# Dense expert product of the peer layers: 512 columns of the first tokens fetched, and another order of high parts, low parts and slot sums

## The chip, the cores and the metric

The program runs on one core of one Trainium2 chip. A core has five engines with queues of their own: TensorE (PE; its weight loads are shown as PEld), VectorE (DVE), ScalarE (ACT), GpSimd (POOL) and SyncE (SP), which mostly starts transfers. Sixteen DMA engines move data between the chip's main memory and the core's on-chip memory. The metric is the device time of one execution in microseconds (us); less is better.

## What is computed

The model is a transformer of four blocks on 256 tokens of 1024 numbers: attention with a mixture of experts, a linear recurrence, a first peer layer, a second attention, and a second peer layer. The change is in the peer layers, which run twice. Cut to what matters:

```
def retrieve_chunk(xc):                                   # 128 tokens
    ...                                                   # product keys choose 8 heads x 16 experts of 16384
    expert = e1 * PEER_KEYS + e2
    g = jax.nn.softmax(top_s, axis=-1)
    u = jnp.take(expert_u, expert, axis=0)
    act = jax.nn.gelu(jnp.einsum('thk,td->thk', u, xc))   # a dot product for each chosen expert
    w = (g * act)
    return jnp.einsum('thk,thkd->td', w, jnp.take(expert_v, expert, axis=0))
```

For each token the layer thus adds 128 rows of `expert_v` (16384 rows of 1024 numbers), each with its own weight.

## The kernel before

The function `peer` (L) does one layer. The 256 tokens are two tiles, t = 0 and t = 1, of 128 tokens each (one token on each of 128 partitions). The last stage of the layer is the weighted sum over rows of `expert_v`. It is made in two ways that run side by side.

The dense way: an earlier step (`group`, `build`) has written the weights into `Wt`, for 128 blocks of 128 experts and all 256 tokens, zero where a token did not choose the expert. The loop over the blocks e then multiplies each block's weights with that block's 128 rows of `expert_v` and adds all products up in PSUM, in `dacc`, one for each token tile. So that the product keeps its precision, both factors are split: `K.split` writes a high part on ScalarE (L88) and the rest, the low part, on VectorE (L89), and `dense` (L1942) makes three products, high by high, high weights by low rows, low weights by high rows. `load(e)` starts the transfer of the rows of block e (`vr`, 512 KB, on SP's queue, five blocks ahead); `vparts(e)` makes `vh` and `vl` of them; `wparts(e)` makes `whi` and `wlo` of the weights. `vl` and `vr` share eight buffers of the pool `gp`; `vh`, `whi` and `wlo` have two buffers each in the pool `vp`.

The fetched way: for the first token tile the last DG = 256 of the 1024 columns are left out of the dense product. In their place `slot` fetches, for slot n of 128, the part of the chosen row that belongs to each of the 128 tokens: an indirect transfer `gv`, started by GpSimd (L1693), with the row numbers in `eidh`. `mix` multiplies it by each token's weight and adds it to `gacc`, on VectorE (L1932). So the first token tile has a second matmul of 256 columns beside each of 512.

Each engine runs its instructions in the order in which they are written in the code. A buffer that is used again makes its next writer wait for its last reader. In the loop, the order in the body of block e is: load of e + 5, weights of e + 1, product of e, high and low part of e + 2, one `mix`, and as many `slot` as a count of blocks allows:

```
for e in range(P):
    load(e + AHEAD)
    wparts(e + 1)
    dense(e)
    vparts(e + 2)
    if len(got) > 4 or got and not todo:
        mix()
    while todo and (P - len(todo)) * (P - 12) < (e + 1) * P:
        slot()
```

After the loop the slots that are left are mixed, and `close` multiplies `gacc` and `dacc` by the layer's `gate` (L1947) and adds them to the tokens `x` (L1949).

Of the kernel before, what the change touches and what calls it, by code (L numbers as in the profile page):

```python
# [1378 lines left out]
AHEAD = 5  # L1379
DG = 256  # L1380


def peer(K, L):
    nc, io, sp, tc = K.nc, K.io, K.sp, K.tc
    pre = f"l{L}_peer_"
    with ExitStack() as ctx:
        gp = K.pool(ctx, "gp", 8, side="right")
        fp = K.pool(ctx, "pp")
        px = K.pool(ctx, "px", space=PSUM)
        R = ExitStack()  # L1390
# [151 lines left out]
        ef = rp.tile([P, TK], F32, name="ef")  # L1542
        dots = fp.tile([P, PH, TK], F32, name="dots")
        act = fp.tile([P, 2, PH, TK], F32, name="act")
        ts = fp.tile([P, 2, PH, TK], F32, name="ts")

# [114 lines left out]
        def softmax(t):  # L1661
            d = act[:, t]
            g = ts[:, t]
            nc.vector.tensor_tensor(out=d, in0=g, in1=g[:, :, 0:1].to_broadcast([P, PH, TK]), op=ALU.subtract)
            nc.scalar.activation(g, d, AF.Exp)
            yield
            sm = fp.tile([P, PH], F32, name=f"psm{t}")
            nc.vector.reduce_sum(sm, g, axis=AX.X)
            nc.vector.reciprocal(sm, sm)
            nc.vector.tensor_tensor(out=g, in0=g, in1=sm[:, :, None].to_broadcast([P, PH, TK]), op=ALU.mult)  # L1670
# [3 lines left out]
        def slots(t, w):  # L1674

            e12 = fp.tile([P, 2, P], I32, tag="e12", name="e12")
            f12 = fp.tile([P, 2, PH, TK], F32, tag="f12", name="f12")
            e_ = eid[:, t].rearrange("p a b -> p (a b)")
# [4 lines left out]
            for i, x in enumerate((f12[:, 0], f12[:, 1], w)):  # L1683
                nc.tensor.transpose(ps[:, i, :], x.rearrange("p a b -> p (a b)"), K.ident)
            eT[t] = fp.tile([P, 3, P], F32, name=f"eT{t}")
            nc.scalar.activation(eT[t], ps, AF.Copy)
            e1b[t] = fp.tile([P, P], BF16, name=f"e1b{t}")
            nc.vector.tensor_copy(e1b[t], ps[:, 0])
            ne2[t] = fp.tile([P, P], F32, name=f"ne2{t}")
            nc.vector.tensor_scalar(ne2[t], ps[:, 1], -1.0, None, op0=ALU.mult)  # L1690
# [31 lines left out]

        eidT = fp.tile([P, P], I32, name="eidT")

# [73 lines left out]

        iof = fp.tile([P, P], F32, name="iof")
        nc.gpsimd.iota(iof, pattern=[[1, P]], base=0, channel_multiplier=0, allow_small_or_imprecise_dtypes=True)  # L1800
        io4 = fp.tile([P, P, 4], BF16, name="io4")
        nc.vector.tensor_copy(io4, iof[:, :, None].to_broadcast([P, P, 4]))
# [85 lines left out]
        def vparts(e):  # L1888

            if e < P and e not in his:  # L1890
                his[e] = vp.tile([P, D], F32R, tag="vh", name="vh")
                lo = gp.tile([P, D], F32R, tag="g", name="vl")
                K.split(his[e], lo, rows_[e])
                rows_[e] = lo
# [11 lines left out]
        O.close()  # L1906
        X.close()
        vp = K.pool(ctx, "vp", 2)
        for e in range(2):
            vparts(e)  # L1910


        table = io[pre + "v_2"].rearrange("r (a c) -> (r a) c", c=DG)
        eidh = fp.tile([P, PH, TK], I32, name="eidh")
        nc.vector.tensor_scalar(eidh, eid[:, 0], float(D // DG), float(D // DG - 1), op0=ALU.mult, op1=ALU.add)
        gacc = vp.tile([P, DG], F32, tag="gacc", name="gacc", bufs=1)
# [115 lines left out]
```

## Time and profile before

| | |
|---|---|
| time, median of 3 runs | 2474.07 us (2470.46 to 2477.63) |
| the profiled execution | 2463.86 us, span 2462.1 us |
| busy share of the span | PE 80%, PEld 61%, DVE 71%, ACT 46%, POOL 37% |
| DMA | 673.56 MB, mean 274 GB/s |
| dense stretch, first layer | from 1122.05 us (first matmul of L1942) |
| dense stretch, second layer | to 2448.7 us (start of its last matmul) |

A span is the time from the first to the last instruction of the program. An engine counts as busy while one of its instructions runs; for TensorE instructions overlap, so that its busy share is no measure of how full it is. In rows of the trace "out<-in" names the tile that is written and those that are read, without buffer numbers, "x128" is a count, and what stands behind "<-" at the end of a row is what ended the idle time ahead of it.

### The profile page before, as it was taken

What the parts mean: (1) busy time and instruction counts of PE and PEld (TensorE: products, weight loads), DVE (VectorE), ACT (ScalarE), POOL (GpSimd) and SP (SyncE); (2) the same over time, 40 slices, a digit from 0 to 9 for tenths busy, and PEclk for the clock granted to TensorE, in tenths of its full rate; (3) what the DMA queues carried; (4) which work ended last, traced back from release to release, by engine and by line L of the source; (5) the groups of instructions that cost most, each with busy time, mean ns of one, the idle gap of its engine ahead of it and who ended that gap; (6) DMA issues with size and microseconds to landing.
All of it is one profiled execution on the core that took longest, in us unless ns stands there. A gap on an engine that the chain in (4) does not pass through costs nothing.

```text
span 2462.1 us, 32882 instructions
## 1 busy us (share of the span) xinstructions
PE 1972.2 (80%) x10819; PEld 1499.6 (61%) x10819; DVE 1748.3 (71%) x4122; ACT 1128.2 (46%) x2320; POOL 900.9 (37%) x951
## 2 busy tenths in 40 slices
PE   6997777777884647779999979987555777899997
PEld 3664333356774545557777756866555555677776
DVE  4663121556688979997777775657898999777776
ACT  4451000246412228885555543552222788655553
POOL 2000000100157766763333330005777667333333
PEclk9998888898897779999999989999887989999999
DMA  8649999673678888997888868328888999788885
GB/s 313 215 169 376 419 419 419 197 249 115 190 264 289 304 301 321 347 351 240 255 254 256 256 222 313 134 91 294 278 315 281 337 339 351 255 256 256 256 255 189
DMA packets 203820, 673.56 MB, mean 274 GB/s; under 512 B 23292, under 2 KB 57064, under 8 KB 187258
## 3 DMA queue, kind: packets, MB, share of 16 engines
q1 hardware_dynamic: 112264, 363.92, 42.3%
q0 software_dynamic: 88672, 304.83, 36.1%
q10 hardware_dynamic: 2706, 2.64, 0.3%
q8 instruction: 87, 1.43, 0.2%
q14 instruction: 91, 0.75, 0.1%
HBM read 668.74 MB, written 1.12 MB: 272 GB/s over the span
## 4 chain that ended last, share of the span: by engine, by line
PE 42%; DVE 19%; issue 8%; ACT 6%; DMA 3%; POOL 2%; another core or an unknown queue 1%; ACTq 1%; DVEq 0%; POOLq 0%; SPq 0%
PE dacc L1942 26%; DVE gu L1869 6%; DVE gu L1764 3%; PE gdot L1754 2%; PE pq L1478 2%; POOL gu L1693 2%; DMA gu<-in_l_peer_u_dram,eid 1%; PE wps L1830 1%; DVE o L1815 1%; DMA w<-in_l_ffn_mod_w_dram 1%; PE facc L94 1%; PE facc L96 1%; PE facc L95 1%; PE md L888 1%
## 5 line engine op out<-in xcount | busy, mean ns | idle before, releaser
L89 DVE TENSOR_TENSOR vl<-vr,vh 128x1024 fp32r<-128x1024 f32 x256 | 313.6, 1226 | 170.2 <-ACT vh L88 162.4
L88 ACT ACTIVATE vh<-vr 128x1024 fp32r<-128x1024 f32 x256 | 271.2, 1060 | 308.8 <-PE dacc L1942 307.7
L1693 POOL DMA_INDIRECT gv<-in_l_peer_v_dram,eidh x256 | 245.6, 959 | 446.9 <-DVE gacc L1932 383.0
L1693 POOL DMA_INDIRECT gu<-in_l_peer_u_dram,eidT x256 | 268.1, 1047 | 123.0 <-DVE gu L1869 61.0
L1942 PE MATMUL dacc<-vh,wlo 128*128 128x512 f32 (+1 forms) x1024 | 311.8, 386 | 0.3
L1693 POOL DMA_INDIRECT gu<-in_l_peer_u_dram,eid x256 | 245.4, 958 | 180.9 <-issue 42.2
L1869 DVE SCALAR_TENSOR_TENSOR gu<-gu,xb 128x1024 f32<-128x1024 f32 x256 | 305.7, 1213 | 7.0 <-remote 3.6
L1942 PE MATMUL dacc<-vh,whi 128*128 128x512 f32 (+1 forms) x1024 | 292.1, 366 | 5.8 <-ACT whi L88 5.8
L1942 PE MATMUL dacc<-vl,whi 128*128 128x512 f32 (+1 forms) x1024 | 291.4, 365 | 0.0
L1764 DVE SCALAR_TENSOR_TENSOR gu<-gu,xr 128x1024 f32<-128x1024 f32 x176 | 212.2, 1209 | 19.3 <-DMA gu<-in_l_peer_u_dram,eid 14.8
L1830 PE MATMUL wps<-ow,o 128*128 128x128 f32 x1024 | 158.1, 303 | 74.2 <-ACT o L1826 63.0
L1942 PEld LDWEIGHTS dacc<-vh,wlo 128*128 128x128 f32 x1024 | 172.7, 188 | 71.1 <-DVE wlo L89 37.7
L1830 PEld LDWEIGHTS wps<-ow,o 128*128 128x128 f32 x1024 | 145.7, 211 | 108.8 <-ACT o L1826 85.9
L1754 PE MATMUL gdot<-h,gT 128*128 128x128 f32 x704 | 122.8, 346 | 109.6 <-ACT gT L1749 50.9
L1838 PE MATMUL xb<-x,pair 128*128 128x512 f32 x512 | 181.3, 466 | 22.7 <-DVE gu L1869 13.6
L1942 PEld LDWEIGHTS dacc<-vh,whi 128*128 128x128 f32 x1024 | 175.1, 189 | 39.3 <-ACT whi L88 6.3
L1942 PEld LDWEIGHTS dacc<-vl,whi 128*128 128x128 f32 x1024 | 174.7, 189 | 33.7
L89 DVE TENSOR_TENSOR ws<-w,ws 128x1024 fp32r<-128x1024 f32 (+1 forms) x104 | 120.9, 1176 | 96.1 <-ACT ws L88 96.1
L1754 PEld LDWEIGHTS gdot<-h,gT 128*128 128x128 f32 x704 | 113.5, 253 | 119.3 <-ACT gT L1749 60.0
L764 PE MATMUL gu<-w,XG 128*32 128x256 f32 x1024 | 93.8, 471 | 49.1 <-DMA w<-in_w_up_dram 27.2
L1838 PEld LDWEIGHTS xb<-x,pair 128*128 128x128 f32 x512 | 93.8, 213 | 55.9 <-DVE gu L1869 27.5
L1932 DVE SCALAR_TENSOR_TENSOR gacc<-gv,act,gacc 128x256 f32<-128x256 f32 x254 | 121.5, 479 | 0.9 <-DMA gv<-in_l_peer_v_dram,eidh 0.6
(533 smaller groups left out, 3790.6 us busy)
## 6 DMA issues: line engine op xcount, KB each, us to landing
vr<-in_l_peer_v_dram SPq DMA_DIRECT2D x256, 512.0 KB
w<-in_w_gate_dram SPq DMA_DIRECT2D x32, 1024.0 KB
w<-in_w_up_dram SPq DMA_DIRECT2D x32, 1024.0 KB
w<-in_w_down_dram SPq DMA_DIRECT2D x32, 1024.0 KB
w<-in_l_mix_mod_w_dram SPq DMA_DIRECT2D x24, 1024.0 KB
w<-in_l_ffn_mod_w_dram SPq DMA_DIRECT2D x24, 1024.0 KB
w<-in_l_peer_q_w_dram SPq DMA_DIRECT2D x16, 1024.0 KB
w<-in_l_fox_in_w_dram SPq DMA_DIRECT2D x16, 1024.0 KB
```

Source lines behind the costliest of these rows:

```text
L88: self.nc.scalar.activation(hi, x, AF.Copy)
L89: self.nc.vector.tensor_sub(lo, x, hi.bitcast(F32))
L764: nc.tensor.matmul(gu[s:s + CAP, j * 256:j * 256 + 256], x[:, k, s:s + CAP], W[n, r][:, k, :], start=k == 0, stop=k == 7, tile_position=(0 ...
L1478: nc.tensor.matmul(ps[:, i, c], qw[n][:, k, i * P:i * P + P], h[:, k, c], start=k == 0, stop=k == 7)
L1693: nc.gpsimd.indirect_dma_start(out=dst, out_offset=None, in_=table, in_offset=bass.IndirectOffsetOnAxis(ap=idx, axis=0))
L1754: nc.tensor.matmul(ps, gT[:, k, :], h[:, k, 0:P], start=k == 0, stop=k == 7)
L1764: nc.vector.scalar_tensor_tensor(g_, g_, 1.0, xr[0], op0=ALU.mult, op1=ALU.mult, accum_out=d)
L1830: nc.tensor.matmul(ps[:, q, :], o2[:, q], ow1[:, q], start=True, stop=True)
L1838: nc.tensor.matmul(ps[:, q:q + 512], K.pair[:, j % 64:j % 64 + 1].to_broadcast([P, P]), x1[j // 64][:, q:q + 512], start=True, stop=True)
L1869: nc.vector.scalar_tensor_tensor(g, g, 1.0, xb.pop(0), op0=ALU.mult, op1=ALU.mult, accum_out=dT[:, j:j + 1])
L1932: nc.vector.scalar_tensor_tensor(gacc, g, w, gacc, op0=ALU.mult, op1=ALU.add)
L1942: nc.tensor.matmul(acc[t][:, q, :n], l[:, c], r[:, 512 * q:512 * q + n], start=e == 0 and i == 0, stop=e == P - 1 and i == 2)
```

## The change

DG becomes 512. The first token tile then needs the dense product for its first 512 columns alone, so its second matmul falls away (`if n:`), and each fetched piece, `gv` and `gacc` are twice as wide. `vh` gets three buffers, and the loop makes the parts of block e + 3 in place of e + 2. In the loop `mix` and `slot` stand ahead of `vparts`; a new function `mixed` spreads the 128 mixes over the blocks 2 to 127, so that none is left behind the loop. Five slots are fetched ahead of the loop. To make room, small tiles whose use ends with the build of the weights move from the pool `fp` to a new pool `fq`, which is closed ahead of `vp`; `eidh` is computed earlier, ahead of that build. The gate is fetched at block 122 instead of 119.

```diff
-DG = 256
+DG = 512
@@
-                his[e] = vp.tile([P, D], F32R, tag="vh", name="vh")
+                his[e] = vp.tile([P, D], F32R, tag="vh", name="vh", bufs=3)
@@
         O.close()
         X.close()
+        F.close()
         vp = K.pool(ctx, "vp", 2)
-        for e in range(2):
-            vparts(e)
-
 
         table = io[pre + "v_2"].rearrange("r (a c) -> (r a) c", c=DG)
-        eidh = fp.tile([P, PH, TK], I32, name="eidh")
-        nc.vector.tensor_scalar(eidh, eid[:, 0], float(D // DG), float(D // DG - 1), op0=ALU.mult, op1=ALU.add)
@@
                         n = 512 - (DG if q > t else 0)
-                        nc.tensor.matmul(acc[t][:, q, :n], l[:, c], r[:, 512 * q:512 * q + n], start=e == 0 and i == 0, stop=e == P - 1 and i == 2)
+                        if n:
+                            nc.tensor.matmul(acc[t][:, q, :n], l[:, c], r[:, 512 * q:512 * q + n], start=e == 0 and i == 0, stop=e == P - 1 and i == 2)
@@
+        def mixed(e):
+
+            return max(e - 1, 0) * P // (P - 2)
+
+        for _ in range(5):
+            slot()
+        for e in range(3):
+            vparts(e)
         wparts(0)
         for e in range(P):
             load(e + AHEAD)
             wparts(e + 1)
             dense(e)
-            vparts(e + 2)
-            if len(got) > 4 or got and not todo:
+            for _ in range(mixed(e) - mixed(e - 1)):
                 mix()
-            while todo and (P - len(todo)) * (P - 12) < (e + 1) * P:
-                slot()
-            if e == P - 9:
+                if todo:
+                    slot()
+            vparts(e + 3)
+            if e == P - 6:
                 gate = gate_rows(K, f"l{L}_ffn", gp.tile([P, D], F32, tag="g", name="gate"))
-        while got:
-            mix()
```

How this moves instructions is seen best on VectorE in the steady part of the loop, first layer. Before, with the numbers of the tiles (`vl` is the low part of rows, `wlo` that of weights, `gacc` the slot sum):

```order
L1932 SCALAR_TENSOR_TENSOR gacc_10702<-gv_10757,act_7116,gacc_10702 128x256
L89 TENSOR_TENSOR wlo_10885<-Wt_8737,whi_10884 128x256
L89 TENSOR_TENSOR vl_10901<-vr_10807,vh_10900 128x1024
L1932 SCALAR_TENSOR_TENSOR gacc_10702<-gv_10781,act_7116,gacc_10702 128x256
L89 TENSOR_TENSOR wlo_10910<-Wt_8737,whi_10909 128x256
L89 TENSOR_TENSOR vl_10926<-vr_10832,vh_10925 128x1024
```

The same place of the changed program:

```order
L1932 SCALAR_TENSOR_TENSOR gacc_10698<-gv_10703,act_7119,gacc_10698 128x512
L89 TENSOR_TENSOR vl_10806<-vr_10746,vh_10805 128x1024
L89 TENSOR_TENSOR wlo_10812<-Wt_8740,whi_10811 128x256
L1932 SCALAR_TENSOR_TENSOR gacc_10698<-gv_10705,act_7119,gacc_10698 128x512
L89 TENSOR_TENSOR vl_10828<-vr_10765,vh_10827 128x1024
L89 TENSOR_TENSOR wlo_10834<-Wt_8740,whi_10833 128x256
```

The slot sum has moved from behind `vl` to ahead of it, so that `wlo` follows `vl` at once, and it is twice as wide.

On TensorE, one block of the product before (`dacc_10703` belongs to the first token tile, `dacc_10704` to the second; x2 are two equal rows, for the two halves of the columns):

```order
L1942 MATMUL dacc_10703<-vh_10692,whi_10705 128x512
L1942 MATMUL dacc_10703<-vh_10692,whi_10705 128x256
L1942 MATMUL dacc_10703<-vl_10693,whi_10705 128x512
L1942 MATMUL dacc_10703<-vl_10693,whi_10705 128x256
L1942 MATMUL dacc_10703<-vh_10692,wlo_10706 128x512
L1942 MATMUL dacc_10703<-vh_10692,wlo_10706 128x256
L1942 MATMUL dacc_10704<-vh_10692,whi_10705 128x512 x2
L1942 MATMUL dacc_10704<-vl_10693,whi_10705 128x512 x2
L1942 MATMUL dacc_10704<-vh_10692,wlo_10706 128x512 x2
```

One block of the changed program:

```order
L1943 MATMUL dacc_10699<-vh_10711,whi_10723 128x512
L1943 MATMUL dacc_10699<-vl_10712,whi_10723 128x512
L1943 MATMUL dacc_10699<-vh_10711,wlo_10724 128x512
L1943 MATMUL dacc_10700<-vh_10711,whi_10723 128x512 x2
L1943 MATMUL dacc_10700<-vl_10712,whi_10723 128x512 x2
L1943 MATMUL dacc_10700<-vh_10711,wlo_10724 128x512 x2
```

The three matmuls of 256 columns are gone, and nine of 512 are left.

At the head of the stage, VectorE before had two low parts and the index product ahead of the first `wlo`:

```order
L89 TENSOR_TENSOR vl_10693<-vr_10659,vh_10692 128x1024
L89 TENSOR_TENSOR vl_10697<-vr_10661,vh_10696 128x1024
L1915 TENSOR_SCALAR eidh_10700<-eid_7113 128x128
L89 TENSOR_TENSOR wlo_10706<-Wt_8737,whi_10705 128x256
L89 TENSOR_TENSOR wlo_10712<-Wt_8737,whi_10711 128x256
```

The changed program has three low parts there:

```order
L89 TENSOR_TENSOR vl_10712<-vr_10664,vh_10711 128x1024
L89 TENSOR_TENSOR vl_10716<-vr_10666,vh_10715 128x1024
L89 TENSOR_TENSOR vl_10720<-vr_10668,vh_10719 128x1024
L89 TENSOR_TENSOR wlo_10724<-Wt_8740,whi_10723 128x256
L89 TENSOR_TENSOR wlo_10730<-Wt_8740,whi_10729 128x256
```

The first `wlo` now stands behind one more low part, and the index product has moved to an earlier stage.

## Rows read from the trace of the kernel before

**Rows 1.** The page, part 4: the chain that ended last, by line.
```profile
PE dacc L1942 26%; DVE gu L1869 6%; DVE gu L1764 3%; PE gdot L1754 2%; PE pq L1478 2%; POOL gu L1693 2%; DMA gu<-in_l_peer_u_dram,eid 1%; PE wps L1830 1%; DVE o L1815 1%; DMA w<-in_l_ffn_mod_w_dram 1%; PE facc L94 1%; PE facc L96 1%; PE facc L95 1%; PE md L888 1%
```

**Rows 2.** Windows: length, busy of PE, PEld, DVE, ACT, POOL, clock, DMA share, GB/s.
```profile
1300.00:1400.00 100.00, 100.00 (x468) 78.94 (x467) 75.96 (x118) 53.28 (x78) 36.85 (x39) 1.00 0.84 256
```

**Rows 3.** Groups from 1150 to 1430 us: count, busy us, mean ns, idle before.
```profile
L89 DVE TENSOR_TENSOR vl<-vr,vh 128x1024 fp32r<-128x1024 f32 x109 | 133.6, 1225 | 67.3 <-ACT vh L88 65.4 <-issue 2.0
...
L88 ACT ACTIVATE vh<-vr 128x1024 fp32r<-128x1024 f32 x110 | 116.6, 1060 | 132.9 <-PE dacc L1942 132.9
...
L1693 POOL DMA_INDIRECT gv<-in_l_peer_v_dram,eidh x110 | 104.4, 949 | 178.7 <-DVE gacc L1932 175.4 <-issue 3.3
...
L1932 DVE SCALAR_TENSOR_TENSOR gacc<-gv,act,gacc 128x256 f32<-128x256 f32 x109 | 52.1, 478 | 0.0
```

**Rows 4.** Timeline around 1300 us: start, duration, engine, line, idle before.
```profile
1300.79 1.06 ACT L88 ACTIVATE vh<-vr 128x1024 fp32r<-128x1024 f32 x1 [1.18 <-PE dacc L1942]
...
1301.89 1.22 DVE L89 TENSOR_TENSOR vl<-vr,vh 128x1024 fp32r<-128x1024 f32 x1 [0.59 <-ACT vh L88]
...
1303.03 0.48 DVE L1932 SCALAR_TENSOR_TENSOR gacc<-gv,act,gacc 128x256 f32<-128x256 f32 x1
1303.19 0.51 PE L1942 MATMUL dacc<-vh,whi 128*128 128x512 f32 x2
...
1303.43 0.42 DVE L89 TENSOR_TENSOR wlo<-Wt,whi 128x256 fp32r<-128x256 f32 x1
1303.53 0.51 PE L1942 MATMUL dacc<-vl,whi 128*128 128x512 f32 x2
...
1303.90 0.62 PE L1942 MATMUL dacc<-vh,wlo 128*128 128x512 f32 x2
...
1304.36 0.64 PE L1942 MATMUL dacc<-vh,whi 128*128 128x512 f32 x2
...
1305.30 0.63 PE L1942 MATMUL dacc<-vh,wlo 128*128 128x512 f32 x2
...
1305.97 1.06 ACT L88 ACTIVATE vh<-vr 128x1024 fp32r<-128x1024 f32 x1 [1.22 <-PE dacc L1942]
```

**Rows 5.** The page, part 5: two wider forms, from the stage before.
```profile
L1693 POOL DMA_INDIRECT gu<-in_l_peer_u_dram,eidT x256 | 268.1, 1047 | 123.0 <-DVE gu L1869 61.0
...
L1869 DVE SCALAR_TENSOR_TENSOR gu<-gu,xb 128x1024 f32<-128x1024 f32 x256 | 305.7, 1213 | 7.0 <-remote 3.6
```

**Rows 6.** Windows of full transfers: first row loads, gathered 4 KB rows, weight loads.
```profile
1112.00:1116.00 4.00, 3.36 (x23) 2.65 (x21) 3.93 (x8) 3.27 (x11) 0.00 (x0) 1.00 0.97 387
1000.00:1050.00 50.00, 37.84 (x204) 29.50 (x205) 49.73 (x100) 44.13 (x134) 35.73 (x34) 0.93 0.97 350
246.00:308.00 62.00, 45.63 (x366) 21.32 (x366) 10.35 (x20) 4.29 (x10) 0.00 (x0) 0.82 1.01 419
```

**Rows 7.** Timeline at the head of the first layer's dense stage.
```profile
1119.70 1.99 ACT L88 ACTIVATE vh<-vr 128x1024 fp32r<-128x1024 f32 x2
1120.78 2.36 DVE L89 TENSOR_TENSOR vl<-vr,vh 128x1024 fp32r<-128x1024 f32 x2 [3.48 <-ACT vh L88]
...
1123.67 1.01 PE L1942 MATMUL dacc<-vh,wlo 128*128 128x512 f32 x2
```

**Rows 8.** Timeline at the end of the second layer's dense stage.
```profile
2448.42 0.62 PE L1942 MATMUL dacc<-vh,wlo 128*128 128x512 f32 x2
2449.82 0.48 DVE L1932 SCALAR_TENSOR_TENSOR gacc<-gv,act,gacc 128x256 f32<-128x256 f32 x1 [0.35 <-DMA gv<-in_l_peer_v_dram,eidh]
2450.34 0.42 DVE L1947 TENSOR_TENSOR gacc<-gacc,gate 128x256 f32<-128x256 f32 x1
2450.68 2.21 DVE L1947 TENSOR_TENSOR gtmp<-dacc,gate 128x512 f32<-128x512 f32 x4
...
2452.81 0.87 DVE L1949 TENSOR_TENSOR x<-gacc,x 128x256 f32<-128x256 f32 x1
2453.60 1.28 DVE L1949 TENSOR_TENSOR x<-gtmp,x 128x512 f32<-128x512 f32 x2
```

More of the change, by code (lines that the diff above doesn't have):

```diff
@@ L1388, in peer @@
         fp = K.pool(ctx, "pp")
+        F = ExitStack()
+        fq = K.pool(F, "fq", side="right")
         px = K.pool(ctx, "px", space=PSUM)
@@ L1542, in peer @@
         ef = rp.tile([P, TK], F32, name="ef")
-        dots = fp.tile([P, PH, TK], F32, name="dots")
+        dots = fq.tile([P, PH, TK], F32, name="dots")
         act = fp.tile([P, 2, PH, TK], F32, name="act")
-        ts = fp.tile([P, 2, PH, TK], F32, name="ts")
+        ts = fq.tile([P, 2, PH, TK], F32, name="ts")
         def top16(jobs):
@@ L1666, in softmax @@
             yield
-            sm = fp.tile([P, PH], F32, name=f"psm{t}")
+            sm = fq.tile([P, PH], F32, name=f"psm{t}")
             nc.vector.reduce_sum(sm, g, axis=AX.X)
@@ L1674, in slots @@
         def slots(t, w):
-            e12 = fp.tile([P, 2, P], I32, tag="e12", name="e12")
-            f12 = fp.tile([P, 2, PH, TK], F32, tag="f12", name="f12")
+            e12 = fq.tile([P, 2, P], I32, tag="e12", name="e12")
+            f12 = fq.tile([P, 2, PH, TK], F32, tag="f12", name="f12")
             e_ = eid[:, t].rearrange("p a b -> p (a b)")
@@ L1684, in slots @@
                 nc.tensor.transpose(ps[:, i, :], x.rearrange("p a b -> p (a b)"), K.ident)
-            eT[t] = fp.tile([P, 3, P], F32, name=f"eT{t}")
+            eT[t] = fq.tile([P, 3, P], F32, name=f"eT{t}")
             nc.scalar.activation(eT[t], ps, AF.Copy)
-            e1b[t] = fp.tile([P, P], BF16, name=f"e1b{t}")
+            e1b[t] = fq.tile([P, P], BF16, name=f"e1b{t}")
             nc.vector.tensor_copy(e1b[t], ps[:, 0])
-            ne2[t] = fp.tile([P, P], F32, name=f"ne2{t}")
+            ne2[t] = fq.tile([P, P], F32, name=f"ne2{t}")
             nc.vector.tensor_scalar(ne2[t], ps[:, 1], -1.0, None, op0=ALU.mult)
@@ L1721, in rows @@
                 yield
-        eidT = fp.tile([P, P], I32, name="eidT")
+        eidT = fq.tile([P, P], I32, name="eidT")
         def second():
@@ L1796, in peer @@
         R.close()
-        iof = fp.tile([P, P], F32, name="iof")
+        iof = fq.tile([P, P], F32, name="iof")
         nc.gpsimd.iota(iof, pattern=[[1, P]], base=0, channel_multiplier=0, allow_small_or_imprecise_dtypes=True)
-        io4 = fp.tile([P, P, 4], BF16, name="io4")
+        io4 = fq.tile([P, P, 4], BF16, name="io4")
         nc.vector.tensor_copy(io4, iof[:, :, None].to_broadcast([P, P, 4]))
@@ L1808, in peer @@
         slots(0, act[:, 0])
-        wT[0], wT[1] = eT[0][:, 2], fp.tile([P, P], F32, name="wT1")
-        dT = fp.tile([P, P], F32, name="dT")
+        wT[0], wT[1] = eT[0][:, 2], fq.tile([P, P], F32, name="wT1")
+        dT = fq.tile([P, P], F32, name="dT")
+        eidh = fp.tile([P, PH, TK], I32, name="eidh")
+        nc.vector.tensor_scalar(eidh, eid[:, 0], float(D // DG), float(D // DG - 1), op0=ALU.mult, op1=ALU.add)
         def group(t, j, dve):
@@ L1955, in peer @@
             dense(e)
-            vparts(e + 2)
-            if len(got) > 4 or got and not todo:
+            for _ in range(mixed(e) - mixed(e - 1)):
                 mix()
-            while todo and (P - len(todo)) * (P - 12) < (e + 1) * P:
-                slot()
-            if e == P - 9:
+                if todo:
+                    slot()
+            vparts(e + 3)
+            if e == P - 6:
                 gate = gate_rows(K, f"l{L}_ffn", gp.tile([P, D], F32, tag="g", name="gate"))
-        while got:
-            mix()
         close((0, slice(D - DG, D), gacc, gacc, nc.vector),
               *((t, slice(512 * q, 512 * q + 512 - (DG if q > t else 0)), acc[t][:, q, :512 - (DG if q > t else 0)], gp.tile([P, D], F32, tag="g", name="gtmp")[:, :512 - (DG if q > t else 0)], (nc.gpsimd, nc.vector)[t])
-                for t in range(2) for q in range(2)))
+                for t in range(2) for q in range(2) if DG < 512 or q <= t))
 RATE = 160
```

## The prediction

> **What bounds the kernel now.** I read the page's chain first. The matmuls that sum the dense expert product (L1942) are the largest piece of what ended last [rows 1], and they run in two stretches, one in each peer layer. The windows come next: in a stretch away from both ends TensorE is busy without a gap at full clock (1.00, the 2.4 GHz level), VectorE is busy three quarters of the time, and the DMA engines show a share of 0.84 at 256 GB/s [rows 2]. That looks like a TensorE bound. It isn't one: matmuls overlap, so a busy PE hides waits of the order of a tenth of a microsecond.
>
> The groups of the stretch say more. 109 low parts in 280 us make 280/109 = 2.57 us for a block of 128 experts. ScalarE is idle 133 us of the 280, and all of that ends with a matmul of L1942; VectorE is idle 67 us, nearly all ended by ScalarE's `vh`; GpSimd waits for the slot sums [rows 3]. ScalarE waits for TensorE, VectorE for ScalarE, so the question is whether TensorE waits for VectorE, which would close a ring. The timeline shows it does [rows 4]. One turn, from `vh` of one block to `vh` two blocks on (there are two buffers of `vh`, so the ring carries every other block):
> - `vh` 1300.79 to `vl` 1301.89: 1.10
> - `vl` to the slot sum `gacc` at 1303.03: 1.14
> - `gacc` to `wlo` at 1303.43: 0.40
> - `wlo` (0.42 long) to the first matmul with `wlo` at 1303.90: 0.47
> - from there to the second tile's matmuls at 1304.36: 0.46 (one of 512 columns that had stood waiting, one of 256)
> - 1304.36 to the last pair's start at 1305.30: 0.94 (two pairs of 512)
> - last pair to the next `vh` at 1305.97: 0.67
>
> The sum is 5.18 us for two blocks, 2.59 a block, which is the measured period within 0.02. So the ring sets the pace: end of the product, high part, low part, slot sum, low part of the weights, end of the product two blocks on.
>
> **The steady block after the change.** Three edits touch this ring.
> - *The slot sum moves ahead of the low part.* VectorE now runs `wlo`, `gacc`, `vl`, so between `vl` and the next `wlo` nothing stands: minus 0.40. The sum falls into the time in which VectorE waits for `vh`. It is twice as wide; the same operation took 478 ns on 256 columns [rows 3] and 1213 ns on 1024 [rows 5], 0.957 ns a column, so 512 take 478 + 245 = 723 ns and hold VectorE 0.40 + 0.245 = 0.645. VectorE then needs 1.14 + 0.645 and 0.34 to 0.42 for `wlo` (with or without the 0.08 by which `gacc`'s 0.48 overlapped its successor), 2.13 to 2.21 a block. If that cover were gone (a block under 2.2) it would itself be the bound.
> - *512 columns are fetched.* The 256-column matmuls of the first token tile go, three a block. Without a stall a pair of 512 + 256 takes 1303.53 - 1303.19 = 0.34 and a pair of 512 takes 0.94/2 = 0.47 or, before a break, 0.46, so a 256 costs 0.34 - 0.23 = 0.11. Only the one behind `wlo` lies in the ring: 0.46 becomes 0.35 (from below 0.23, if the waiting matmul loses its start-up; from above 0.46). Minus 0.11.
> - *Three buffers of `vh`, made three blocks ahead.* I cost this at nothing in the ring. The high part of block e+3 still waits for the product of block e, and `wlo` of block e+2 stands behind the low part of block e+3 on VectorE, so the same two-block ring passes through other names. Before, block e+2's own high part was in it; now the part is made a block earlier than needed, but the queue keeps it in.
>
> The new turn: 1.10 + 1.14 + 0.47 + 0.35 + 0.94 + 0.67 = 4.67 us, 2.335 a block, 0.255 less than by the same rows before. Taken from 2.57 it gives 2.31. TensorE alone needs nine matmuls at 0.23 and the start-up, 2.07 + 0.11 = 2.18, so it still waits about 0.13. GpSimd's issue took 949 ns [rows 3] and stays below half the block; I take it unchanged for rows twice as long, because the same instruction for rows of 1024 columns took 1047 ns [rows 5]; it would need 2.31 us to count.
>
> The ring holds some 125 of the 128 blocks, and the first three or four blocks before had no slot sum in it yet, so the gain is 125 x 0.255 - 0.5 = 31.4 us a layer.
>
> **The transfers.** A block brings 512 KB of rows and, now, 128 x 2 KB instead of 128 x 1 KB of gathered rows: 786 KB instead of 655 KB, which in 2.31 us is 340 GB/s. The trace of before has no such mixture at that rate. Nearest rows: 387 GB/s where the first row loads of this very stretch queue up behind gathers, 350 GB/s where gathers of 4 KB rows run alone, 419 for weight loads [rows 6]. I take the first for the row loads and the second for the gathered rows: 524/387 + 262/350 = 1.35 + 0.75 = 2.10 us, under 2.31 by a tenth, hidden. The bounds are 786/419 = 1.88 and, from the share, the second rival. The Trainium skill, "DMA: Bandwidth & Descriptors", section Specifications, speaks against the change here: it gives a core about 358 GB/s from HBM, by which I estimate 2.20 us a block and the same sum with half the margin; the trace's 387 and 419 already lie above that figure.
>
> **Head and tail of each layer.** Three high and low parts now stand ahead of the first weights instead of two. ScalarE's two took 1.99, VectorE's two 2.36, the second of them 1.14 [rows 7]; a third `vl` puts the first `wlo` 1.14 later, and the small index product (0.13 of VectorE's queue there) has moved to the stage before, where it costs about as much as it saves. The first matmul with `wlo` stood at 1123.67; it comes 1.0 later. Bounds: 0.93 (a third high part, 1.99 - 1.06, if ScalarE's work were what counts) and 1.14. The five gathers issued first find GpSimd idle.
>
> At the end, before, the last product pair ended at 2448.42 + 0.62 = 2449.04, but the last slot sum waited for its gather until 2449.82, and the gated sum came at 2450.34; the last add ended at 2454.88, 5.84 behind the product [rows 8]. Now the slot sums end inside the loop and their gating ahead of the product's end; three products of 512 follow (2.21 less the 256 one, about 1.88), the add of the 512 columns (0.87 for 256, plus 0.245), and 1.28 for two adds, with 0.2 of overlap: 4.1. Minus 1.7 a layer; bounds 0.8 (only the wait goes) and 2.5. The gate's load is issued three blocks nearer the end, still some 14 us ahead of its use.
>
> **Sum.** 2 x (31.4 - 1.0 + 1.7) = 64.2 us. The profiled execution took 2463.86 us (its span is 2462.1), so 2399.7. The median of the three runs shown is 2474.07, 10.2 above that execution; the same difference from it gives 2410 us, 2.6% less. About 0.3% (7.4 us) is what a measurement of this kernel tells from no change.
>
> **The rivals.**
> - *The ring opens, and VectorE sets the pace.* If the stall's start-up goes with the stall (0.23 in place of 0.35) and the two interleaved rings fall in step, the block comes down to VectorE's 2.13 to 2.21. At 2.17 it saves 0.40 x 251 + 1.4 = 102 us: 2372. For it: the turn is only 0.15 above that floor. Against: nothing in the order takes `vl` out from ahead of `wlo`.
> - *The transfers set the pace, and it ends slower.* The place is the wait of `vh` for its rows. If the share of 0.84 at 256 GB/s [rows 2] were work that doesn't overlap, the engines would give 256/0.84 = 305 GB/s and a block need 786/305 = 2.58 us, about level with before. A little less, 300 GB/s, makes 2.62: 0.05 x 252 + 2 for the heads = 15 us more, with nothing left of the tail's gain because the last gathers come late: 2489. It decides from where the mixture gets less than 786/2.57 = 306 GB/s. For it: the share is high while nobody waits for a transfer. Against: 387 GB/s at a share of 0.97 [rows 6], so a share overstates what a transfer needs.
> - *Between the two:* the mixture gets 306 to 340 GB/s, most of the gain is lost. At 320, 2.46 a block, it saves 0.11 x 251 + 1 = 29: 2445.
> - *No change:* the ring is longer by another wait that the rows don't show (the `gacc` of 512 holding VectorE so long that `vl` comes late, 1.0 instead of 0.645): 2.52 and more, some 2460 to 2480.
>
> **How the numbers follow.** The forecast has 0.62, with a block of 2.25 to 2.38 and its own range 2392 to 2426. The opened ring 0.11, transfers in between 0.13, slower by transfers 0.09, no change 0.05. The range leaves out the slower end and the deepest part of the first rival: 2375 to 2452. Faster by over 0.3%: 0.62 + 0.11 + 0.13 + 0.01 of the last = 0.87; within 0.3%: 0.04; slower 0.09.
>
> **What would show it.** In the windows of the dense stretch 43 low parts in 100 us instead of 39, the clock still at 1.00, DMA at about 340 GB/s. In the timeline `wlo` directly behind `vl`, `gacc` behind `wlo`, ended before the next `vh` is. ScalarE's `vh` should still be released by a matmul: that is the ring. If `vh` is released by the transfer of its rows, or `gacc` by its gather, the second or third rival has come. If VectorE has no idle time ahead of `vl`, the first has. At the end, the gated sum should stand ahead of the last matmul. The prediction is wrong above all if the mixture of row loads and gathers doesn't reach 340 GB/s.

## The result and the profile after

The changed kernel takes 2404.84 us (median of 4 runs, 2401.21 to 2416.12); the kernel before, run on the same chip, 2472.27. The ratio is 0.9733, with a 95% interval of 0.9696 to 0.977: 2.7% faster, where 2.6% was forecast. Its profiled execution took 2404.95 us with a span of 2403.2, so the profiled spans differ by 58.9 us.

The windows of the changed kernel: length, busy time of PE, PEld, DVE, ACT, POOL, granted clock, DMA share, GB/s. The first two lie at the head of the first layer's dense stage, the third well inside it; 2230 to 2330 us in the second layer shows the same (VectorE 94%, 341 GB/s).

```profile
1120.00:1125.00 5.00, 1.17 (x3) 0.50 (x2) 3.33 (x3) 4.04 (x6) 3.91 (x3) 0.50 0.48 139
1125.00:1130.00 5.00, 4.55 (x12) 3.52 (x12) 0.83 (x3) 1.05 (x2) 3.06 (x3) 0.50 0.97 340
1300.00:1390.00 90.00, 86.31 (x349) 62.29 (x349) 84.69 (x117) 52.90 (x78) 50.47 (x39) 1.00 0.97 340
```

Beside [rows 2], VectorE went from 76% busy to 94%, the transfers from 256 to 340 GB/s, and PE from 100% to 96%: with less work to cover it, the wait for the low part of the weights is now seen as idle time of the multiplying engine. The page says so too. This is its chain by line; in [rows 1] the product had 26% of it.

```profile
PE dacc L1943 10%; DVE gu L1873 7%; ACT vh L88 5%; DVE gu L1766 4%; DVE wlo L89 2%; PE gdot L1756 2%; PE pq L1480 2%; DVE o L1819 1%; DMA w<-in_l_ffn_mod_w_dram 1%; PE facc L94 1%; ACT ow L1828 1%; DMA gu<-in_l_peer_u_dram,eid 1%; POOL gu L1695 1%; PE facc L96 1%
```

The groups of the changed kernel from 1150 to 1390 us, which answer to [rows 3]: 104 low parts in 240 us are 2.31 us a block (one part more or less at an edge is 0.02). ScalarE still waits for the product alone and the weight load for `wlo`: the ring is still there. VectorE's idle time ahead of `vl` fell from 67 us in 280 to 14 in 240.

```profile
L1695 POOL DMA_INDIRECT gv<-in_l_peer_v_dram,eidh x105 | 138.2, 1316 | 105.5 <-DVE gacc L1932 101.6 <-DVE wlo L89 3.1 <-issue 0.6
L89 DVE TENSOR_TENSOR vl<-vr,vh 128x1024 fp32r<-128x1024 f32 x104 | 127.8, 1229 | 14.3 <-ACT vh L88 14.3
...
L88 ACT ACTIVATE vh<-vr 128x1024 fp32r<-128x1024 f32 x103 | 109.3, 1061 | 99.8 <-PE dacc L1943 99.8
...
L1943 PEld LDWEIGHTS dacc<-vh,wlo 128*128 128x128 f32 x309 | 57.8, 187 | 52.1 <-DVE wlo L89 43.0
```

One turn of that ring, from the timeline of the changed kernel (start, duration, engine, idle time before it), as in [rows 4]:

```profile
1300.76 1.21 DVE L89 TENSOR_TENSOR vl<-vr,vh 128x1024 fp32r<-128x1024 f32 x1
...
1301.10 1.69 POOL L1695 DMA_INDIRECT gv<-in_l_peer_v_dram,eidh  x1 [1.58 <-DVE gacc L1932]
...
1302.14 1.06 ACT L88 ACTIVATE vh<-vr 128x1024 fp32r<-128x1024 f32 x1 [1.16 <-PE dacc L1943]
...
1303.23 1.26 DVE L89 TENSOR_TENSOR vl<-vr,vh 128x1024 fp32r<-128x1024 f32 x1 [0.27 <-ACT vh L88]
1303.24 0.95 POOL L1695 DMA_INDIRECT gv<-in_l_peer_v_dram,eidh  x1 [0.45 <-DVE gacc L1932]
...
1304.42 0.41 DVE L89 TENSOR_TENSOR wlo<-Wt,whi 128x256 fp32r<-128x256 f32 x1
1304.75 0.74 DVE L1932 SCALAR_TENSOR_TENSOR gacc<-gv,act,gacc 128x512 f32<-128x512 f32 x1
1304.88 0.50 PE L1943 MATMUL dacc<-vh,wlo 128*128 128x512 f32 x1 [0.19 <-DVE wlo L89]
1305.22 0.62 PE L1943 MATMUL dacc<-vh,whi 128*128 128x512 f32 x2
...
1306.15 0.62 PE L1943 MATMUL dacc<-vh,wlo 128*128 128x512 f32 x2
...
1306.80 1.06 ACT L88 ACTIVATE vh<-vr 128x1024 fp32r<-128x1024 f32 x1 [1.16 <-PE dacc L1943]
```

`vh` to `vl` 1.09, `vl` to `wlo` 1.19, `wlo` to the first matmul with it 0.46, to the second tile's matmuls 0.34, to the last pair 0.93, to the next `vh` 0.65: 4.66 us for two blocks. The forecast had 1.10, 1.14, 0.47, 0.35, 0.94 and 0.67, 4.67. `gacc` stands directly behind `wlo`, and in one block of two `vl` still waits (0.27) for its high part, in the other (1300.76, 1305.42) it follows `gacc` at once. So VectorE is idle for only 0.27 of the 4.66: its own limit lies just below the ring.

The head of the first layer's dense stage, timeline of the changed kernel:

```profile
1120.59 2.94 ACT L88 ACTIVATE vh<-vr 128x1024 fp32r<-128x1024 f32 x3
...
1123.88 0.80 PE L1943 MATMUL dacc<-vh,whi 128*128 128x512 f32 x1 [3.83 <-ACT whi L88]
...
1125.55 0.80 PE L1943 MATMUL dacc<-vh,wlo 128*128 128x512 f32 x1 [0.45 <-DVE wlo L89]
1126.14 1.06 PE L1943 MATMUL dacc<-vh,whi 128*128 128x512 f32 x2
...
1127.00 1.06 PE L1943 MATMUL dacc<-vl,whi 128*128 128x512 f32 x2
...
1128.95 1.06 ACT L88 ACTIVATE vh<-vr 128x1024 fp32r<-128x1024 f32 x1 [4.81 <-PE dacc L1943]
```

And the first high part that a product released in the kernel before, from its timeline at the same place, with one of its windows there (columns as above):

```profile
1126.41 1.06 ACT L88 ACTIVATE vh<-vr 128x1024 fp32r<-128x1024 f32 x1 [4.11 <-PE dacc L1942]
...
1125.00:1130.00 5.00, 5.00 (x26) 4.19 (x25) 1.62 (x3) 2.52 (x4) 4.01 (x4) 0.98 0.55 176
```

From the first `vh` to the first matmul with `wlo` is now 4.96 us; in [rows 7] it was 3.97. To the end of the first product it is 8.36, where it was 1126.41 - 1119.70 = 6.71.

The end of the second layer's dense stage in the changed kernel, which answers to [rows 8]:

```profile
2389.49 2.32 DVE L1932 SCALAR_TENSOR_TENSOR gacc<-gv,act,gacc 128x512 f32<-128x512 f32 x3
...
2391.84 0.69 DVE L1948 TENSOR_TENSOR gacc<-gacc,gate 128x512 f32<-128x512 f32 x1
2391.94 0.61 PE L1943 MATMUL dacc<-vh,wlo 128*128 128x512 f32 x2
2392.45 1.88 DVE L1948 TENSOR_TENSOR gtmp<-dacc,gate 128x512 f32<-128x512 f32 x3
...
2394.25 0.79 DVE L1950 TENSOR_TENSOR x<-gacc,x 128x512 f32<-128x512 f32 x1
2394.96 1.28 DVE L1950 TENSOR_TENSOR x<-gtmp,x 128x512 f32<-128x512 f32 x2
```

The slot sums and their gating are done before the product ends at 2392.55; the last add ends 3.69 us later, where it was 5.84.

By stages, from the starts and ends in the two timelines (dense: first `vh` to the end of the last matmul; tail: from there to the last add):

| us | before | after | difference |
|---|---|---|---|
| dense, first layer | 332.97 | 304.62 | -28.4 |
| dense, second layer | 332.79 | 303.63 | -29.2 |
| two tails | 11.61 | 7.38 | -4.2 |
| all the rest | | | +2.8 |
| span | 2462.1 | 2403.2 | -58.9 |

The rest lies outside the dense stages and tails, where the change moves little but the index product; whether these 2.8 us are its doing or the spread between two executions, no run shows.

### The profile page after: what moved, and what is told of

The parts are those of the page before. It is cut to its first block, busy times and chain, and to the rows that moved or that the text cites. A ratio compares the mean times of both kernels' runs of the same rounds, so it can differ in the third digit from the quotient of the medians.

```text
span 2403.2 us, 31336 instructions
## 1 busy us (share of the span) xinstructions
PE 1893.5 (79%) x10051; PEld 1396.2 (58%) x10051; DVE 1809.0 (75%) x4120; ACT 1129.1 (47%) x2320; POOL 990.2 (41%) x949
## 4 chain that ended last, share of the span: by engine, by line
PE 25%; DVE 23%; issue 14%; ACT 12%; DMA 3%; POOL 2%; another core or an unknown queue 2%; ACTq 1%; DVEq 0%; SPq 0%; POOLq 0%
PE dacc L1943 10%; DVE gu L1873 7%; ACT vh L88 5%; DVE gu L1766 4%; DVE wlo L89 2%; PE gdot L1756 2%; PE pq L1480 2%; DVE o L1819 1%; DMA w<-in_l_ffn_mod_w_dram 1%; PE facc L94 1%; ACT ow L1828 1%; DMA gu<-in_l_peer_u_dram,eid 1%; POOL gu L1695 1%; PE facc L96 1%
## 5 line engine op out<-in xcount | busy, mean ns | idle before, releaser
L1695 POOL DMA_INDIRECT gv<-in_l_peer_v_dram,eidh x256 | 334.1, 1305 | 284.5 <-DVE gacc L1932 231.9
L1943 PE MATMUL dacc<-vh,wlo 128*128 128x512 f32 x768 | 281.3, 420 | 25.3 <-DVE wlo L89 25.3
L1943 PE MATMUL dacc<-vh,whi 128*128 128x512 f32 x768 | 262.1, 395 | 7.7 <-ACT whi L88 7.7
L1943 PE MATMUL dacc<-vl,whi 128*128 128x512 f32 x768 | 261.3, 394 | 0.0
L1943 PEld LDWEIGHTS dacc<-vh,wlo 128*128 128x128 f32 x768 | 144.5, 188 | 129.3 <-DVE wlo L89 106.2
L1932 DVE SCALAR_TENSOR_TENSOR gacc<-gv,act,gacc 128x512 f32<-128x512 f32 x254 | 188.1, 740 | 0.2
L1943 PEld LDWEIGHTS dacc<-vl,whi 128*128 128x128 f32 x768 | 145.2, 189 | 33.6
L1943 PEld LDWEIGHTS dacc<-vh,whi 128*128 128x128 f32 x768 | 145.7, 190 | 30.5 <-ACT whi L88 8.1
```

The source lines that it names most:

```text
L1695: nc.gpsimd.indirect_dma_start(out=dst, out_offset=None, in_=table, in_offset=bass.IndirectOffsetOnAxis(ap=idx, axis=0))
L1932: nc.vector.scalar_tensor_tensor(gacc, g, w, gacc, op0=ALU.mult, op1=ALU.add)
```

## The experiments

My theory is that the pace is the two-block ring: product, high part, low part, low part of the weights, product. The rivals are a plain saving of matmul work (three narrow matmuls less a block), a third buffer that does the work, and transfers that limit the changed kernel. The first four runs were made on one chip, where the kernel before took 2427.75 us (10 runs, 2419.45 to 2433.6), the last four on another, where it took 2426.96 (7 runs, 2420.53 to 2432.34). Ratios are to the kernel before on the same chip, and what a ratio is in microseconds is against its time there. The changed kernel itself was not run on these chips; it enters by its ratio above, 0.9733, whose interval is 0.0037 to either side, so where a difference is small I go by the length of the dense stages and tails in the traces. The first four edits are against the changed kernel.

**The order alone.** 256 columns fetched and two buffers, as before, with the slot sum ahead of the low part. What else the change moves stays as in the changed kernel: the slot sums spread over the blocks, five gathers ahead of the loop, the index product.

```diff
-DG = 512
+DG = 256
-                his[e] = vp.tile([P, D], F32R, tag="vh", name="vh", bufs=3)
+                his[e] = vp.tile([P, D], F32R, tag="vh", name="vh", bufs=2)
-        for e in range(3):
+        for e in range(2):
-            vparts(e + 3)
+            vparts(e + 2)
```

> The slot sum ahead of the low part, but 256 columns fetched and two buffers of the high part, made two blocks ahead. Theory (a ring of two blocks through high part, low part, low part of the weights and product): the turn loses the 0.40 us of the slot sum, 5.18 - 0.40 = 4.78, 2.39 a block; but with twelve matmuls TensorE needs 9 x 0.23 + 3 x 0.11 = 2.40 without a stall and 2.51 with one in every block, so the block comes down from 2.57 to 2.40 to 2.50 only: 20 to 45 us faster than before, 2427 to 2452. Rival (the order makes the whole gain): 2.31 a block, about 2405. Rival (fewer matmuls make it, the order nothing): 2.57, about 2470.

Measured: 2381.99 us, ratio 0.9821 (0.9787 to 0.9855), 45.8 us less, at the upper end of the 20 to 45 expected. Its two tails are 3.87 us each, so some 4 of the 45.8 come from the spread of the slot sums and not from the order. Its window (columns as above):

```profile
1250.00:1350.00 100.00, 100.00 (x497) 84.53 (x496) 81.16 (x125) 56.69 (x84) 41.48 (x43) 1.00 0.87 272
```

and two of its groups from 1150 to 1350 us:

```profile
L89 DVE TENSOR_TENSOR vl<-vr,vh 128x1024 fp32r<-128x1024 f32 x83 | 101.8, 1227 | 37.8 <-ACT vh L88 37.8
...
L1943 PE MATMUL dacc<-vh,wlo 128*128 128x512 f32 x248 | 84.3, 394 | 0.0
```

A block takes 200/83 = 2.41 us, and no matmul with `wlo` waits: the ring would now allow (5.18 - 0.40)/2 = 2.39, and twelve matmuls, nine of them 0.23 and three 0.11, need 2.40. The order brings the ring down to what TensorE has to do, where it ends.

**Everything but the order.** 512 columns and three buffers, with the low part ahead of the slot sum again.

```diff
+            vparts(e + 3)
             for _ in range(mixed(e + 1) - mixed(e)):
                 ...
-            vparts(e + 3)
```

> The changed kernel with the slot sum put back behind the low part of the rows; 512 columns and three buffers stay. Theory: the sum of 512 holds VectorE 0.67 us between the low part of the rows and that of the weights, so the two-block turn grows from 4.66 to 5.33, 2.66 a block: 0.35 x 250 = 87 us slower than the changed kernel, about 2490, slower than before by some 20. Rival (three buffers have opened the ring, so the place of the sum counts for nothing): 2.31 a block, about 2405. Rival (nine matmuls in place of twelve are what pays): at most 2.4 a block, about 2430.

Measured: 2440.29 us, ratio 1.0056 (1.0038 to 1.0075): slower than before, by 12.5 us where some 20 were expected. Its window:

```profile
1250.00:1350.00 100.00, 85.85 (x339) 60.38 (x337) 83.97 (x115) 51.41 (x75) 36.42 (x38) 1.00 0.90 300
```

and its groups from 1150 to 1350 us:

```profile
L89 DVE TENSOR_TENSOR vl<-vr,vh 128x1024 fp32r<-128x1024 f32 x76 | 93.2, 1226 | 32.4 <-ACT vh L88 32.4
L1943 PE MATMUL dacc<-vh,wlo 128*128 128x512 f32 x227 | 84.5, 426 | 25.3 <-DVE wlo L89 25.3
```

200/76 = 2.63 us a block. TensorE has three matmuls fewer than in the kernel before and is slower: the longer sum (0.66 from its start to that of `wlo`, instead of 0.40) stands between `vl` and `wlo`, and the ring waits for it. A plain saving of matmul work, as the whole of the gain, falls with this run. PE now shows 14% of idle time where the kernel before, with nearly the same pace, showed none.

**Two buffers.** The changed kernel with the high parts made two blocks ahead.

```diff
-                his[e] = vp.tile([P, D], F32R, tag="vh", name="vh", bufs=3)
+                his[e] = vp.tile([P, D], F32R, tag="vh", name="vh", bufs=2)
-        for e in range(3):
+        for e in range(2):
-            vparts(e + 3)
+            vparts(e + 2)
```

> The changed kernel with two buffers of the high part, made two blocks ahead; order and 512 columns stay. Theory: the two-block turn has the same parts, high part, low part, low part of the weights, product, so 2.31 a block as in the changed kernel; the head of each layer is shorter by one low part, 1.0 us and up to 1.6 with the clock's later rise: 2 to 3 us faster, 2402 and within 0.3% of it. Rival (the third buffer pays): the block goes back by a good part of the 0.26 gained, 2.45 and more, 2440 and above.

Measured: 2358.55 us, ratio 0.9726 (0.9693 to 0.9759), as the changed kernel's 0.9733. A dense stage and its tail together take 307.8 us in the first layer and 307.4 in the second, 308.3 and 307.3 in the changed kernel: the shorter head that was expected is there, but the tail is 1.0 longer. Groups from 1150 to 1350 us:

```profile
L89 DVE TENSOR_TENSOR vl<-vr,vh 128x1024 fp32r<-128x1024 f32 x86 | 106.1, 1234 | 11.3 <-ACT vh L88 11.3
...
L1943 PEld LDWEIGHTS dacc<-vl,whi 128*128 128x128 f32 x257 | 48.1, 187 | 34.7 <-DVE vl L89 22.2
```

2.32 us a block. The weight load now waits mostly for `vl` instead of `wlo`, but the turn is as long. The third buffer brings nothing in this change.

**The weights' parts two blocks ahead.** If `wlo` behind the low part is what holds the ring closed, it opens when each `wlo` is made a block earlier.

```diff
-                ws[e] = [vp.tile([P, T], F32R, tag=n, name=n) for n in ("whi", "wlo")]
+                ws[e] = [vp.tile([P, T], F32R, tag=n, name=n, bufs=3) for n in ("whi", "wlo")]
         wparts(0)
+        wparts(1)
-            wparts(e + 1)
+            wparts(e + 2)
```

> The changed kernel with the parts of the weights made two blocks ahead (three buffers of each), so that the low part of the weights of block e+3 and not e+2 stands behind the low part of the rows of block e+3. Theory: the ring now spans three blocks and its turn of about 4.7 us makes 1.6 a block, so it no longer counts; VectorE sets the pace with 1.14 + 0.33 + 0.67 = 2.14 us a block, TensorE needs 2.07: 2.15 to 2.2 a block, 28 to 40 us faster than the changed kernel, 2365 to 2377. Rival (the transfers are the limit already, the DMA share in the changed kernel is 0.96 to 0.97 at 338 GB/s): 2.31 a block stays, about 2405.

Measured: 2315.94 us, ratio 0.954 (0.9508 to 0.9572). That is 0.0193 x 2427 = 47 us below the changed kernel, more than the 28 to 40 expected. Its window:

```profile
1250.00:1350.00 100.00, 100.00 (x424) 75.46 (x423) 100.00 (x141) 63.99 (x95) 85.66 (x48) 1.00 0.99 368
```

its groups from 1150 to 1350 us:

```profile
L1695 POOL DMA_INDIRECT gv<-in_l_peer_v_dram,eidh x95 | 172.4, 1814 | 29.0 <-issue 28.4 <-DMA gv<-in_l_peer_v_dram,eidh 0.6
L89 DVE TENSOR_TENSOR vl<-vr,vh 128x1024 fp32r<-128x1024 f32 x94 | 115.4, 1227 | 0.0
L1943 PE MATMUL dacc<-vh,wlo 128*128 128x512 f32 x282 | 100.3, 410 | 0.0
```

and its timeline on VectorE:

```profile
1251.05 0.42 DVE L89 TENSOR_TENSOR wlo<-Wt,whi 128x256 fp32r<-128x256 f32 x1
...
1251.38 0.75 DVE L1932 SCALAR_TENSOR_TENSOR gacc<-gv,act,gacc 128x512 f32<-128x512 f32 x1
...
1252.04 1.22 DVE L89 TENSOR_TENSOR vl<-vr,vh 128x1024 fp32r<-128x1024 f32 x1
...
1253.18 0.42 DVE L89 TENSOR_TENSOR wlo<-Wt,whi 128x256 fp32r<-128x256 f32 x1
```

VectorE runs without a gap: 0.33 + 0.66 + 1.14 = 2.13 us a block, and no matmul or weight load waits for `wlo`. The ring is open and VectorE sets the pace, at the lower end of the 2.13 to 2.21 that the first rival had. It costs something at the end: VectorE is late there, and the tail is 5.5 us instead of 3.7.

**VectorE or the transfers.** The version with the weights two blocks ahead, with the slot sum over 64 of the 512 fetched columns; everything is still fetched.

```diff
+        nc.vector.memset(gacc, 0.0)
-                nc.vector.tensor_scalar(gacc, g, w, None, op0=ALU.mult)
+                nc.vector.tensor_scalar(gacc[:, :64], g[:, :64], w, None, op0=ALU.mult)
-                nc.vector.scalar_tensor_tensor(gacc, g, w, gacc, op0=ALU.mult, op1=ALU.add)
+                nc.vector.scalar_tensor_tensor(gacc[:, :64], g[:, :64], w, gacc[:, :64], op0=ALU.mult, op1=ALU.add)
```

> The kernel with the weights two blocks ahead, and the slot sum over 64 of its 512 columns (the other 448 columns of the first tokens' fetched part are left out of the result; all rows are still fetched). VectorE then needs about 1.14 + 0.33 + 0.25 = 1.7 us a block. Theory (in that kernel VectorE is the limit, and the transfers at 370 GB/s are not): TensorE takes over with nine matmuls at 0.23, 2.07 to 2.1 a block in place of 2.13, and the transfers reach 375 to 380 GB/s: 8 to 15 us faster, ratio to the kernel before 0.948 to 0.951. Rival (the transfers are the limit, their share is 0.99 to 1.00): the block stays at 2.13 and the ratio at 0.954.

Measured: 2291.38 us, ratio 0.9454 (0.9426 to 0.9482), below what was expected. Its window:

```profile
1250.00:1350.00 100.00, 100.00 (x443) 82.81 (x442) 85.94 (x148) 66.96 (x98) 80.60 (x51) 1.00 1.01 389
```

and its groups from 1150 to 1350 us (the product is L1944 here):

```profile
L88 ACT ACTIVATE vh<-vr 128x1024 fp32r<-128x1024 f32 x98 | 104.0, 1062 | 66.0 <-PE dacc L1944 50.3 <-DMA vr<-in_l_peer_v_dram 13.1 <-DVE gacc L1933 1.5
...
L1944 PE MATMUL dacc<-vh,wlo 128*128 128x512 f32 x295 | 98.8, 389 | 0.0
```

200/98.5 = 2.03 us a block, with no wait on TensorE: nine matmuls at 0.226, its own floor. The same row loads and gathers come at 389 GB/s, so in the version before it VectorE was the limit and the transfers were not. The waits of `vh` for its rows grow here to 13 of its 66 us, from 4 of 73.

**A slower gather issue: the slot sum in PSUM.** GpSimd's issue grew from 949 ns [rows 3] to 1316 in the changed kernel and 1814 with the weights ahead. I suspected the slot sum, whose operands both lie in SBUF, the core's on-chip memory; this run puts `gacc` into PSUM, in the version with the weights two blocks ahead.

```diff
-        gacc = vp.tile([P, DG], F32, tag="gacc", name="gacc", bufs=1)
+        gacc = K.pool(ctx, "pg", space=PSUM).tile([P, DG], F32, name="gacc")
```

> The kernel with the weights two blocks ahead, and the slot sum kept in PSUM, so that its instruction reads one operand and not both from SBUF. GpSimd's issue of a gather took 949 ns before the change, 1305 after it and 1814 with the weights two ahead, while VectorE's busy share of the dense stretch went 0.76, 0.94, 1.00; in the stage before, with VectorE as busy but one operand in PSUM, it took 1050. Theory (the issue stands behind VectorE instructions that read both operands from SBUF): the sum's 0.67 of 2.14 us no longer holds it, and the mean issue falls to between 1.2 and 1.6 us; the block is VectorE's and stays at 2.13 to 2.17, ratio 0.954 within 0.003. Rival (the issue is slow because the transfer queues are full): it stays at 1.8.

Measured: 2311.73 us, ratio 0.9528 (0.9503 to 0.9553), not told apart from 0.954; the issue fell to 1732 ns only. Its group from 1150 to 1350 us and two rows of its timeline:

```profile
L1695 POOL DMA_INDIRECT gv<-in_l_peer_v_dram,eidh x95 | 164.6, 1732 | 36.0 <-DVE gacc L1932 21.7 <-issue 14.3
...
1250.54 1.22 DVE L89 TENSOR_TENSOR vl<-vr,vh 128x1024 fp32r<-128x1024 f32 x1
...
1250.91 1.68 POOL L1695 DMA_INDIRECT gv<-in_l_peer_v_dram,eidh  x1 [0.45 <-DVE gacc L1932]
```

The issue that begins 0.37 into a `vl` ends 0.83 behind that `vl`'s end. The expectation is missed: the slot sum's operands are at most a small part of it. What holds the issue is the low part of the rows. In the run with the sum over 64 columns the issues begin at many different points of a `vl`, as this one, 0.68 into it:

```profile
1273.87 1.22 DVE L89 TENSOR_TENSOR vl<-vr,vh 128x1024 fp32r<-128x1024 f32 x1
...
1274.55 1.37 POOL L1695 DMA_INDIRECT gv<-in_l_peer_v_dram,eidh  x1 [0.30 <-issue]
```

It too ends 0.83 behind. Those in that run's dense stretches that begin 0.05 to 1.0 into a `vl` take from 1.99 down to 1.03 us, and all end 0.80 to 0.83 behind it; those that begin together with a `vl`, or between two, take 0.95. Full transfer queues, the rival, would not follow `vl` like this. One case stays open: with the weights two blocks ahead many issues begin 0.55 into a `vl`, take 1.82 and end 1.15 behind it.

The run settles another rival too. In the version with the weights two blocks ahead an issue of 1.81 and a pause of 0.30 before it fill nearly all of GpSimd's 2.13 a block, so GpSimd might have set the pace there. Here it waits for slot sums again, 21.7 us in 200, and the block is as long.

**Weights ahead, two buffers.** The edit is made on the version with the weights two blocks ahead. Is the third buffer idle there too?

```diff
-                his[e] = vp.tile([P, D], F32R, tag="vh", name="vh", bufs=3)
+                his[e] = vp.tile([P, D], F32R, tag="vh", name="vh", bufs=2)
-        for e in range(3):
+        for e in range(2):
-            vparts(e + 3)
+            vparts(e + 2)
```

> The weights two blocks ahead, but two buffers of the rows' high part, made two blocks ahead. Theory (each ring alone is enough): the high and the low part of block e+2 still wait for the product of block e, and its second product group needs that low part: 1.09 + 1.28 + 0.35 + 0.23 + 0.94 + 0.67 = 4.56 us for two blocks, 2.28 a block, about as the changed kernel: ratio 0.968 to 0.974. So the third buffer would count here, where it counted for nothing in the changed kernel. Rival (only the weights' low part behind the rows' low part held the ring): 2.13 a block, ratio 0.954.

Measured: 2346.36 us, ratio 0.9668 (0.9642 to 0.9695), a little under the 0.968 to 0.974 expected; 200/88 = 2.27 us a block, where 2.28 was worked out. Two of its groups from 1150 to 1350 us:

```profile
L89 DVE TENSOR_TENSOR vl<-vr,vh 128x1024 fp32r<-128x1024 f32 x88 | 107.5, 1222 | 7.6 <-ACT vh L88 7.5
...
L1943 PEld LDWEIGHTS dacc<-vl,whi 128*128 128x128 f32 x264 | 49.4, 187 | 39.4 <-DVE vl L89 31.5
```

The ring is closed again, through `vl`. The third buffer is worth 31 us here (0.9668 against 0.954) and nothing without the weights ahead: only the two together open it.

**A shorter head.** The version with the weights two blocks ahead, with the third high and low part behind the first two of the weights.

```diff
-        for e in range(3):
+        for e in range(2):
             vparts(e)
         wparts(0)
         wparts(1)
+        vparts(2)
```

> The kernel with the weights two blocks ahead, and at the head of the stage the third high and low part of rows made behind the first weights. Theory: the first product with the low part of the weights starts 1.0 us earlier in each layer, and the clock rises earlier: dense stage 1.0 to 1.7 us shorter in each, ratio 0.9525 to 0.9535, within what can be told from 0.954. Rival (the head's cost only shifts into the first blocks): the stage stays at 279 us from its first high part to its last matmul.

Measured: 2309.9 us, ratio 0.9524 (0.9493 to 0.9555). From the first `vh` to the first matmul with `wlo` it takes 3.9 us in either layer instead of 5.0. The dense stages are 0.8 and 1.2 us shorter (278.0 and 278.3 against 278.8 and 279.5), where 1.0 to 1.7 was expected; two layers of one run differ by 0.8 themselves. So the earlier start is shown, and the gain only roughly; the whole time can't tell it from 0.954. The weights two blocks ahead, alone, with the shorter head or with the sum in PSUM, make the fastest versions that still sum everything.

## Why the prediction was right

**The ring.** Right, and in its pieces: 4.66 us measured for 4.67 worked out. The runs bear out its two edits apart: the order takes 0.40 out of the turn, but with twelve matmuls only down to TensorE's 2.40; without the order the wider fetch loses. The order alone saves 46 us and the rest alone loses 12.5, while both together, by the ratio, are worth 0.0267 x 2427 = 65 (each of the three has the shorter tails, some 4 us): the three narrow matmuls less pay only where the ring lets them.

**The step to the gain.** Slightly off. I took 0.255 from the period of 2.57 and got 2.31. From the end of the first product to the last matmul of the first layer there are 127 blocks: before (332.97 - 6.71)/127 = 2.569, after (304.62 - 8.36)/127 = 2.333. The turn by itself, 4.67/2 = 2.335, was the better forecast; carrying the old 0.02 along was the error. It makes 127 x 0.236 = 30.0 us instead of 31.4.

**The third buffer at nothing.** Right in the changed kernel; two buffers give the same ratio. The reason given is shown by the two runs with the weights ahead: `wlo` behind the later low part kept the buffer from counting.

**The transfers.** Hidden, as forecast: 340 GB/s at a share of 0.97, and from 1150 to 1390 us no `vh` or slot sum waits for one (in both layers together one `vh` does, for 0.8). The second rival's point of decision, 306 GB/s as the most that the engines give, is refuted by 368 and 389 GB/s with the same mixture. The Trainium skill's figure of about 358 GB/s ("DMA: Bandwidth & Descriptors", Specifications) is passed as well, as it was in [rows 6].

**The head.** Mis-sized. The first matmul with `wlo` came 0.99 later (1.0 forecast), but the first product ended 1.65 later. TensorE had stood idle for 3.8 us ahead of its first matmul here, and the windows show it at 0.50, the 1.2 GHz level, from 1120 to 1130 us, and by then the first product is over: a pair took 0.86 there, where it takes 0.46 at full clock. The kernel before stood at 0.50 too from 1120 to 1125 us, but from 1125 to 1130 its window shows 0.98, so the end of its first product ran at full clock. In the first 20 us of the stage the mean granted clock was 0.86 before and is 0.76 now. The term left out this second delay, 0.65 a layer.

**The tail.** Mis-sized: 2.1 us a layer instead of 1.7. Three products take 1.88 as forecast, but the add of the 512 columns takes 0.79, not 0.87 + 0.245.

**GpSimd's issue unchanged.** Wrong: 949 ns became 1316. The width, which I had looked at, is not the reason, the order is: the slot sum that lets a gather go now ends ahead of `vl`, and every other issue begins inside one. It cost nothing, since GpSimd still waits for the slot sums about 1 us a block.

**The sum.** 64.2 was forecast; the dense stages and tails gave 57.5 + 4.2 = 61.7, of which the rest of the profiled execution took 2.8 back. The two executions differ by 58.9 and the medians by 67.4, so the stages were forecast to within 2.5 us. The errors of a layer partly cancel (step 1.4 and head 0.65 too favourable, tail 0.4 too small), and the closeness of 2404.84 to 2410 beyond that is luck.

**The rivals.** VectorE as the pace did not come about, for the reason given against it; it came close, with 14.3 of 240 us idle, and one edit more makes it so. In between, slower and no change did not come either. (The block of the no-change rival adds up to (4.67 + 0.355)/2 = 2.51, not 2.52.)

## What to carry to other kernels

A TensorE that shows as 100% busy can still be in a ring with two other engines: add up one turn in the timeline, with every in-order queue that stands between a result and its user, and see whether it equals the period. Shortening the turn by reordering one queue is worth up to the next floor (here TensorE's 2.40, then VectorE's 2.13, then TensorE's 2.03), and work cut off the ring is worth nothing or less. A further buffer counts only when nothing else in the ring's queues ties it to the same block: here it was worth 31 us with the weights' parts ahead and nothing without.

## What the runs showed that I had not expected

- GpSimd's issue of a gather of 2 KB rows takes either about 0.95 or about 1.69 us in the changed kernel, in turn from block to block. The short one began within 0.01 us of a `vl`, the long one 0.34 into it, and that decides: an issue that begins inside a `vl` mostly ends about 0.82 us behind it, wherever in it it began (some end 1.15 behind, as said above). The width of the rows is not the reason: with the slot sum behind the low part the same gathers took 952 ns. Why an issue waits for a `vl` that it began beside stays open.
- One core drew 389 GB/s from a mixture of 512 KB row loads and gathers of 2 KB rows, at a share of 1.01; 340 GB/s showed as 0.97, and 256 as 0.84. The share says little about what is left.
